# The first stage of four SwiGLU channel mixers by seven block products for eight, with the residual kept in DRAM between phases

## The chip, the cores and the metric

One Trainium2 chip, one core of it. The time is that of the device for one execution of the whole kernel, in microseconds (us); lower is better. TensorE (PE) multiplies, VectorE (DVE) and ScalarE (ACT) work element by element, GpSimd (POOL) does small things, and SyncE's queue (SP) issues the transfers between DRAM and the on-chip memory (SBUF). Products are summed in eight PSUM banks of 128 x 512 fp32.

## What is computed

Two layers of a trunk, each with a channel mixer, a token mixer and a second channel mixer. 640 tokens (512 latent, 128 context), width 1024, feed-forward width 2816:

```python
def _swiglu(x, w1, w3, w2):
    return (jax.nn.silu(x @ w1) * (x @ w3)) @ w2

def _layer(x, mod, l, norm_g, ffn_w1, ffn_w3, ffn_w2, mixer):
    sh1, sc1, g1, sh2, sc2, g2, sh3, sc3, g3 = jnp.split(mod[:, None, :].astype(x.dtype), N_MOD, axis=-1)
    h = _modulate(_rmsnorm(x, norm_g[l, 0]), sh1, sc1)
    x = x + 0.5 * g1 * _rmsnorm(_swiglu(h, ffn_w1[l, 0], ffn_w3[l, 0], ffn_w2[l, 0]), norm_g[l, 1])
    h = _modulate(_rmsnorm(x, norm_g[l, 2]), sh2, sc2)
    y, st = mixer(h)          # layer 0: recurrent (RG-LRU); layer 1: means over windows (pool)
    x = x + g2 * _rmsnorm(y, norm_g[l, 3])
    h = _modulate(_rmsnorm(x, norm_g[l, 4]), sh3, sc3)
    x = x + 0.5 * g3 * _rmsnorm(_swiglu(h, ffn_w1[l, 1], ffn_w3[l, 1], ffn_w2[l, 1]), norm_g[l, 5])
```

`mod` is a product of the conditioning vectors with a 1024 x 9216 matrix per layer. The weights are fp32 and are read once.

## The kernel before

The program is six phases in a row: FFN(0,0), RG(0,1), FFN(0,2), FFN(1,0), pool(1,1), FFN(1,2). FFN(l,s) is a channel mixer. The program is one stream of instructions for each engine, in the order in which the Python code writes them; engines wait for one another where data or buffers ask for it, and nothing reorders within an engine.

Every fp32 product is three products of the format fp32r: each operand is split into a high part (`wh`, `hh`, `gh`, a copy by ACT) and a low part (`wl`, `hl`, `gl`, a subtraction by DVE), and low x high, high x low and high x high are summed. Weights come in pieces of 128 x 1024 (512 KB) into two `raw` buffers and are split in `ensure` (ACT L137, DVE L138) into six `wh` and six `wl` slots, in the order in which they are used.

A channel mixer goes over 22 blocks of 128 feed-forward features. For a block, `ffn_A` makes u (with w1) and v (with w3), with the features on the 128 partitions, for token group A (256 tokens, bank `uvA`) and group B (384 tokens, banks `uB`, `vB`): eight input slices of 128, three products each (`mmA`, L326). `ffn_post` takes the silu of u (ACT) and multiplies by v (DVE, L347); `put_g` splits the result (L153, L154). After two blocks, `block_B` does the second stage with w2: five token tiles x two halves of the output, six products of 512 columns each into one of three `b` banks (`mmB`, L366), evacuated by DVE into `yacc` (L374). This is always one pair behind the first stage. The last four blocks are done tile by tile in `final`: behind each tile's last product come its norm, the residual `x` (`c_res`: L291, L292), the next phase's norm, transposes (PE L431), modulation (ACT L439, DVE L437) and the split into `hhA/hlA` (tiles 0 and 1) and `hhB/hlB` (tiles 2 to 4). `ffn_start` does the next phase's products for group A while the norms of the last tiles finish.

Between the products, `mod_step` slips in the products of the modulation for coming phases (PE L207, their weights in two `mw` buffers), and with `G` the vectors that scale the residual. `start` is the first phase's beginning, where the modulation comes in four groups of 256 features (PE L842) and products follow as each is there. The residual `x`, 640 x 1024, lies in SBUF; in the RG mixer, whose temporaries take its place, it is stored to DRAM and read back.

Of the kernel before, what the change touches and what calls it, by code (L numbers as in the profile page):

```python
# [16 lines left out]
P = 128  # L17
# [11 lines left out]
NW = 6  # L29
NRAW = 2  # L30
GAP = 2
SMP = TOK - P
XW = TOK + GAP

# Column table: name -> (first column, number of columns).
# [44 lines left out]
PAIRS = {1: (0, 1), 3: (2, 3), 4: (4,)}  # L80


class Kern:
    def __init__(self, ctx, tc, io):
# [8 lines left out]
    BUFS = {"wh": NW, "wl": NW, "raw": NRAW, "mw": 2, "yacc": NT, "gh": 4, "gl": 4,  # L93
            "xp": 1, "xc": 1, "r": 2, "i": 2, "a": 2, "gt": 1, "ab": 2, "G": 1,
            "st": 12, "uvA": 2, "uB": 1, "vB": 1, "b": 3, "m": 1}
# [9 lines left out]
    def init_pieces(self, pieces):  # L105
        self.pieces = pieces
        self.n_dma = 0
        self.n_split = 0
        self.raws = {}
        self.wparts = {}  # L110
        self.cur = 0
        self.limit = len(pieces)
        self.g_on_dve = False

    def dma_upto(self, n):
        while self.n_dma < min(n, len(self.pieces)):
            raw = self.t("raw", [P, D])
            self.nc.sync.dma_start(raw, self.pieces[self.n_dma])
            self.raws[self.n_dma] = raw
            self.n_dma += 1  # L120

    def ensure(self, last):
        last = min(last, self.limit - 1, len(self.pieces) - 1)
        while self.n_split <= last:
            i = self.n_split
            self.dma_upto(i + NRAW)
            raw = self.raws.pop(i)
            if i in self.scaled:
                for k in range(2):
                    rk = raw[:, k * 512:(k + 1) * 512]  # L130
                    self.nc.vector.tensor_mul(rk, rk, self.psc[self.scaled[i]])
            wh = self.t("wh", [P, D], F32R)
            wl = self.t("wl", [P, D], F32R)
            if self.dve_lo <= i < self.dve_hi:
                self.nc.vector.tensor_copy(wh, raw)
            else:
                self.nc.scalar.activation(wh, raw, AF.Copy)  # L137
            self.nc.vector.tensor_sub(wl, raw, wh.bitcast(F32))  # L138
            self.wparts[i] = (wh, wl)
            self.n_split += 1  # L140
        self.dma_upto(self.n_split + NRAW)

    def take(self):
        i = self.cur
        self.ensure(i)
        self.cur += 1
        return self.wparts.pop(i)

    def ahead(self, k=NW):
        self.ensure(self.cur + k - 1)  # L150
# [6 lines left out]
    def mod_init(self):  # L157
# [18 lines left out]
        self.m_use = 0  # L176
        self.ab = {}
# [5 lines left out]
    def mod_dma(self):  # L183
        while self.m_dma < min(self.m_use + 2, len(self.mitems)):
# [75 lines left out]
    def mod_step(self, n=1):  # L260
        for _ in range(n):
            if next(self.gen, "end") in ("hold", "end"):
                return

# [11 lines left out]
    def rstd(self, src):  # L276
        nc = self.nc
        junk = self.t("xp", [P, D], BF16)
# [6 lines left out]

    def c_res(self, t, l, s):
# [4 lines left out]
        nc.vector.scalar_tensor_tensor(y, y, rs, self.G[(l, s)][:, v], op0=ALU.mult, op1=ALU.mult)  # L291
        nc.vector.tensor_add(x, x, y)  # L292

    def c_stat2(self, t):
        self.rs2[t] = self.rstd(self.x[:, t])

    def c_xn(self, t):
        self.nc.scalar.activation(self.y[t], self.x[:, t], AF.Copy, scale=self.rs2[t])  # L298

    def c_T(self, t):  # L300
        self.tp[t] = []
        for h in range(2):
            pt = self.p("uB" if h == 0 else "vB")
            for q in range(4):
                kk = 4 * h + q
                self.nc.tensor.transpose(pt[:, q * P:(q + 1) * P], self.y[t][:, kk * P:(kk + 1) * P], self.col("ident"))
            self.tp[t].append(pt)

    def hsl(self, t):
        g, off = (0, t * P) if t < 2 else (1, (t - 2) * P)  # L310
        return g, slice(off, off + P)

    def new_h(self):
        self.hh = [self.t("hhA", [P, KC, 256], F32R), self.t("hhB", [P, KC, 384], F32R)]
        self.hl = [self.t("hlA", [P, KC, 256], F32R), self.t("hlB", [P, KC, 384], F32R)]
        self.rs2 = {}
        self.tp = {}

# [21 lines left out]
    def ffn_post(self, f, grp, u, v):  # L340
        nc = self.nc
        if grp == 0:
            self.su[f] = self.t("r", [P, XW])
# [678 lines left out]
```

## Time and profile before

| what | value |
|---|---|
| time, three runs | 2300.38, 2300.75, 2301.27 us (median 2300.75) |
| span of the profiled execution | 2297.5 us |
| the profiled execution's own time | not among the three; the median lies 3.25 us above the span |
| mean granted clock of TensorE | 0.992 |
| read from DRAM, written | 238.91 MB, 5.25 MB |

The span runs from the first to the last instruction. "Busy" is the sum of the durations of an engine's instructions where they don't overlap. The chain that ended last is followed back from the last instruction to whatever released it. In a group's row stand count, busy time, mean duration in ns of one, and then the idle time of the engine just ahead of these instructions with what ended most of it. In a timeline, chain or window row the first number is the start in us, the second the length.

### The profile page before, as it was taken

The numbers are of one execution on the slowest core, as the hardware profiler recorded it, in microseconds if no ns is written. First come the engines' busy times: TensorE is split into PE (matmuls) and PEld (weight loads), VectorE is DVE, ScalarE is ACT, GpSimd is POOL, SyncE is SP. The second block draws the span as 40 slices with busy tenths as digits, with TensorE's granted clock in tenths as the row PEclk, the third lists the DMA queues.
The fourth block names the chain that finished last, engine by engine and source line by source line (L and its number), as shares of the span: only waits on it lengthen the run. The fifth ranks groups of instructions, "written<-read, shape, count | busy, mean of one in ns | idle before, by whom it ended". The sixth has DMA issues, their size and how long they took to land.

```text
span 2297.5 us, 32647 instructions
## 1 busy us (share of the span) xinstructions
PE 2243.3 (98%) x14071; PEld 2024.6 (88%) x14071; DVE 1089.0 (47%) x1570; ACT 753.0 (33%) x1123; POOL 64.9 (3%) x107
## 2 busy tenths in 40 slices
PE   7999999998999999999999999999999899999998
PEld 5999889987888898989998898898897799999997
DVE  5333433346998643343344434334436743343444
ACT  5322112226976622112224421212125732222211
POOL 0000000000111000000000000000000100000000
PEclk9999999999999999999999999999999999999999
DMA  8333343324424344332221433433331322222221
GB/s 280 121 115 119 111 128 112 114 74 147 129 101 142 133 133 125 110 124 74 81 68 55 150 108 109 129 119 120 105 111 45 113 76 74 81 68 87 79 74 46
DMA packets 74288, 246.27 MB, mean 107 GB/s; under 512 B 7568, under 2 KB 15776, under 8 KB 74144
## 3 DMA queue, kind: packets, MB, share of 16 engines
q1 hardware_dynamic: 74112, 244.18, 33.6%
q8 instruction: 110, 1.80, 0.3%
q14 instruction: 34, 0.28, 0.0%
q0 software_dynamic: 32, 0.01, 0.0%
HBM read 238.91 MB, written 5.25 MB: 106 GB/s over the span
## 4 chain that ended last, share of the span: by engine, by line
PE 86%; DVE 6%; ACT 5%; DMA 2%; issue 1%; POOL 1%; SPq 0%; POOLq 0%; ACTq 0%; DVEq 0%
PE b L366 23%; PE uvA L326 22%; PE uB L326 17%; PE vB L326 16%; PE m L207 3%; ACT xp L280 2%; DVE yacc L291 1%; DVE x L292 1%; DVE yacc L374 1%; PE b L573 1%; POOL st L283 1%; DMA mw<-in_mod_w_dram 1%; ACT yacc L298 0%; PE b L746 0%; PE m L249 0%
## 5 line engine op out<-in xcount | busy, mean ns | idle before, releaser
L138 DVE TENSOR_TENSOR wl<-raw,wh 128x1024 fp32r<-128x1024 f32 x294 | 356.5, 1223 | 482.3 <-ACT wh L137 482.3
L137 ACT ACTIVATE wh<-raw 128x1024 fp32r<-128x1024 f32 x270 | 281.1, 1055 | 648.1 <-PE b L366 405.8
L326 PE MATMUL uvA<-hhA,wl 128*128 128x256 f32 x1536 | 440.2, 287 | 1.6 <-ACT xp L532 1.5
L326 PE MATMUL uvA<-hlA,wh 128*128 128x256 f32 x1536 | 435.8, 284 | 0.0
L326 PE MATMUL uvA<-hhA,wh 128*128 128x256 f32 x1536 | 435.3, 284 | 0.0
L366 PE MATMUL b<-wh,gl 128*128 128x512 f32 x960 | 376.6, 392 | 3.4 <-DVE gl L154 1.6
L366 PE MATMUL b<-wl,gh 128*128 128x512 f32 x960 | 375.0, 391 | 0.0
L366 PE MATMUL b<-wh,gh 128*128 128x512 f32 x960 | 374.3, 391 | 0.0
L374 DVE TENSOR_TENSOR yacc<-yacc,b 128x512 f32<-128x512 f32 x380 | 256.0, 686 | 169.7 <-PE b L366 169.6
L326 PEld LDWEIGHTS uvA<-hhA,wl 128*128 128x128 f32 x1536 | 294.3, 192 | 21.9 <-issue 15.4
L326 PEld LDWEIGHTS uvA<-hlA,wh 128*128 128x128 f32 x1536 | 294.8, 192 | 2.1 <-DVE hlB L154 0.4
L326 PEld LDWEIGHTS uvA<-hhA,wh 128*128 128x128 f32 x1536 | 294.7, 192 | 1.6 <-issue 1.6
L326 PE MATMUL uB<-hhB,wl 128*128 128x384 f32 x760 | 259.4, 341 | 0.9 <-ACT hhB L153 0.9
L326 PE MATMUL vB<-hhB,wl 128*128 128x384 f32 x760 | 254.8, 335 | 2.3 <-ACT gt L584 2.3
L326 PE MATMUL uB<-hlB,wh 128*128 128x384 f32 x760 | 254.9, 335 | 0.2
L326 PE MATMUL vB<-hhB,wh 128*128 128x384 f32 x760 | 255.0, 336 | 0.0
L326 PE MATMUL vB<-hlB,wh 128*128 128x384 f32 x760 | 254.9, 335 | 0.0
L326 PE MATMUL uB<-hhB,wh 128*128 128x384 f32 x760 | 254.6, 335 | 0.0
L366 PEld LDWEIGHTS b<-wh,gl 128*128 128x128 f32 x960 | 180.2, 188 | 48.0 <-issue 5.8
L366 PEld LDWEIGHTS b<-wh,gh 128*128 128x128 f32 x960 | 180.2, 188 | 37.6
L366 PEld LDWEIGHTS b<-wl,gh 128*128 128x128 f32 x960 | 180.3, 188 | 36.0
L347 DVE TENSOR_TENSOR r<-r,uvA 128x256 f32<-128x256 f32 x88 | 37.0, 421 | 266.6 <-ACT r L346 266.5
(207 smaller groups left out, 2389.5 us busy)
## 6 DMA issues: line engine op xcount, KB each, us to landing
raw<-in_w_dram SPq DMA_DIRECT2D x264, 512.0 KB, 3.5
mw<-in_mod_w_dram SPq DMA_DIRECT2D x132, 512.0 KB, 3.7
raw<-in_w_in_dram SPq DMA_DIRECT2D x16, 512.0 KB, 3.6
raw<-in_w_out_dram SPq DMA_DIRECT2D x8, 512.0 KB, 3.5
x_spill<-x SPq DMA_DIRECT2D x5, 512.0 KB, 2.6
x<-x_spill SPq DMA_DIRECT2D x5, 512.0 KB, 6.7
x<-in_x_s_dram SPq DMA_DIRECT2D x4, 512.0 KB, 6.3
wl<-in_mod_w_dram SPq DMA_DIRECT2D x4, 512.0 KB, 9.0
```

The costliest lines, as they stand in the source:

```text
L137: self.nc.scalar.activation(wh, raw, AF.Copy)
L138: self.nc.vector.tensor_sub(wl, raw, wh.bitcast(F32))
L207: nc.tensor.matmul(ps[32 * j:32 * j + 32, 0:256], self.csil[:, k, :], w[:, j * 256:(j + 1) * 256], start=(k == 0), stop=(k == KC - 1), til ...
L280: nc.scalar.activation(junk, src, AF.Square, scale=1.0 / 32.0, accum_out=ms)
L283: nc.gpsimd.tensor_tensor(rs, ms, self.mhalf, op=ALU.pow)
L291: nc.vector.scalar_tensor_tensor(y, y, rs, self.G[(l, s)][:, v], op0=ALU.mult, op1=ALU.mult)
L292: nc.vector.tensor_add(x, x, y)
L326: self.nc.tensor.matmul(out, a[:, sl], b[g][:, k], start=(n == 0), stop=(n == 3 * KC - 1))
L347: nc.vector.tensor_mul(su[:, cs], su[:, cs], v)
L366: nc.tensor.matmul(pb, a[:, ts_], b[:, ns], start=(c == 0), stop=(c == 3 * len(fl) - 1))
L374: nc.vector.tensor_add(y, y, pb)
L573: nc.tensor.matmul(pb, u[:, ws], v[:, a:b], start=(n == 0), stop=(n == 2))
```

## The change

**The block products.** Two blocks of features are taken together. Tokens are halved (320 and 320, `HT`), input features are halved (512 and 512, `HK` = 4 slices), and the two blocks of a pair are the halves of the output. With A the 2 x 2 blocks of the token matrix and b those of the weight, the four output blocks of u (and of v) come from seven products in Winograd's form of Strassen's algorithm, each of 4 slices x 3 fp32r products of 320 columns: A11 b11, A12 b21, S1 t1, S2 t2, S3 t3, S4 b22, A22 t4, with

    S1 = A21 + A22    S3 = A11 - A21    S2 = S1 - A11    S4 = A12 - S2
    t1 = b12 - b11    t3 = b22 - b12    t2 = b22 - t1    t4 = t2 - b21

(Line numbers of the changed kernel are added behind some lines.) The S are made once a phase, by DVE, and split (`h_sums`, L410 to L413 and L207/L208). The t are made for each weight by DVE (`weight_gen`), and each of the seven operands is split by itself, as a quarter of 128 x 512 (ACT L136, DVE L137), into 11 `wp` slots that hold high and low part together. A weight of a pair now comes as one load of 1 MB; w2 comes in pairs of blocks, 1 MB, split as before (L174, L177). The products are combined by DVE from PSUM.

```diff
+                b11, b12, b22, b21 = (raw[:, n * 512:(n + 1) * 512] for n in range(4))
+                if kind == "full":
+                    yield quarter(b11)
+                T = self.t("T", [P, D])
+                t1, t3 = T[:, 0:512], T[:, 512:D]
+                V.tensor_sub(T, raw[:, 512:1536], raw[:, 0:1024])      # L150
+                t2, t4 = b12, b11
+                V.tensor_sub(t2, b22, t1)                              # L152
+                yield quarter(t2)
+                if kind == "full":
+                    yield quarter(b21)
+                yield quarter(t3)
+                yield quarter(t1)
+                V.tensor_sub(t4, t2, b21)                              # L158
+                yield quarter(t4)
+                yield quarter(b22)
...
+    def h_sums(self, ks, cols):
+        V = self.nc.vector
+        (f11, f12), (f21, f22), s1 = *([x[:, ks, cols] for x in f] for f in self.F), self.fs1[:, ks, cols]
+        V.tensor_add(s1, f21, f22)
+        V.tensor_sub(f21, f11, f21)
+        V.tensor_sub(f11, s1, f11)
+        V.tensor_sub(f12, f12, f11)
+        for n, x in (("S2", f11), ("S3", f21), ("S1", s1), ("S4", f12), ("A22", f22)):
+            hi, lo = self.H[n]
+            self.split(hi[:, ks, cols], lo[:, ks, cols], x)
...
+    def prod(self, out, h, **kw):
+        self.mmP(out, h, self.get(), **kw)      # 12 matmuls, L472
+        self.done()                             # makes the next quarters, as slots allow
+
+    def seven_rest(self, u, s1, tag):
+        V = self.nc.vector
+        c12, c21, c22 = u[:, 1, 0:HT], u[:, 0, HT:TOK], u[:, 1, HT:TOK]
+        p6 = self.bank(tag)
+        self.prod(p6, "S2")
+        V.tensor_add(c12, p6, s1)               # L497
+        yield
+        p7 = self.bank(tag)
+        self.prod(p7, "S3")
+        V.tensor_add(c21, p7, c12)              # L501
+        p5 = self.bank(tag)
+        self.prod(p5, "S1")
+        V.tensor_add(c22, p5, c21)              # L504
+        p4 = self.bank(tag)
+        self.prod(p4, "A22")
+        V.tensor_sub(c21, c21, p4)              # L507
+        self.prod(p5, "S4", onto=True)
+        V.tensor_add(c12, c12, p5)              # L509
+        yield
+
+    def seven(self, u):
+        p1 = self.bank()
+        self.prod(p1, "A11")
+        s1 = u[:, 0, 0:HT]
+        self.nc.scalar.activation(s1, p1, AF.Copy)   # L517
+        it = self.seven_rest(u, s1, "q")
+        next(it)
+        self.prod(p1, "A12", onto=True)
+        next(it)
+        return p1
```

`onto` adds to a bank that holds a sum already. Four `q` banks and three `b` banks take the place of `uvA`, `uB`, `vB` and `b`. `ffn_u` takes the silu (ACT L530 of the first output block, L531 of the other three), `ffn_v` multiplies (DVE L536, L537) and splits g (L207, L208, 1280 elements for the pair). The second stage's matmuls and evacuations (L561) are as before.

**The phases.** `ffn_start` does A11 and A12 of the first two pairs' four weights and copies the results of A11 aside; the other five products of each need all tokens. `ffn_rest` does these (for the first pair into `b` banks), the second stage of the first pair, and from the third pair on the whole:

```diff
+    def ffn_start(self, nxt):
+        self.mod_allow(self.phase_mods[nxt[0:2]])
+        self.ffn_open()
+        for m in range(4):
+            self.prod(self.c11[m], "A11")
+            self.nc.scalar.activation(self.s1[m], self.c11[m], AF.Copy)
+        self.mod_step(5)
+        for m in range(4):
+            self.prod(self.c11[m], "A12", onto=True)
+        self.mod_step(4)
+        self.ahead()
...
+        for b in range(2, NB):
+            u, v = self.ffn_uv(b)
+            self.ffn_u(u, self.seven(u))
+            self.mod_step(2)
+            self.ffn_v(b, u, v, self.seven(v))
+            self.mod_step(2)
+            if b < NB - 1:
+                self.block_B((2 * b - 2, 2 * b - 1), False)
+                self.mod_step(2)
```

**The residual.** `x` has no place in SBUF any more. `c_res` loads a token tile of it from DRAM into one of the two `mw` buffers (a tile ahead), and `c_next` stores it back, in every phase. Because `mw` is shared, `mod_allow` caps how far the modulation runs ahead.

```diff
     def c_res(self, t, l, s):
         nc = self.nc
-        y, x = self.y[t], self.x[:, t]
+        if t == 0:
+            self.xt = {}
+            self.x_load(0)
+        if t + 1 < NT:
+            self.x_load(t + 1)
+        y, x = self.y[t], self.xt[t]
```

RG and pool use the new buffers, and RG takes tokens in groups of 320 and 320 instead of 256 and 384. `start` works in the same four groups of modulation with the new operands.

**The order on the engines.** VectorE in one steady pair of FFN(1,0), from the weights of the pair's first block to that block's g. Before, weight splits (L138) take turns with the multiplications by v (L347) and the split of g (L154):

```order
L138 TENSOR_TENSOR wl_12051<-raw_11968,wh_12050 128x1024
L347 TENSOR_TENSOR r_12041<-r_12041,uvA_11992 128x256
L138 TENSOR_TENSOR wl_12177<-raw_12048,wh_12176 128x1024
L347 TENSOR_TENSOR r_12041<-r_12041,vB_12063 128x384
L138 TENSOR_TENSOR wl_12183<-raw_12054,wh_12182 128x1024
L154 TENSOR_TENSOR gl_12115<-r_12041,gh_12114 128x640
```

One weight split stands ahead of each reader of a bank (`uvA`, `vB`). After, in a steady pair of the same phase, the combinations of u (L501 to L509) stand between weight sums (L150, L152, L158) and splits of quarters (L137) and of w2 (L177):

```order
L137 TENSOR_TENSOR wp_13157<-raw_12874,wp_13157 128x512
L501 TENSOR_TENSOR c_13108<-q_13160,c_13108 128x320
L177 TENSOR_TENSOR wp_13191<-raw_13077,wp_13175 128x1024
L504 TENSOR_TENSOR c_13108<-q_13178,c_13108 128x320
L507 TENSOR_TENSOR c_13108<-c_13108,q_13194 128x320
L150 TENSOR_TENSOR T_13271<-raw_13173 128x1024
L177 TENSOR_TENSOR wp_13222<-raw_13077,wp_13207 128x1024
L509 TENSOR_TENSOR c_13108<-c_13108,q_13178 128x320
L152 TENSOR_TENSOR raw_13173<-raw_13173,T_13271 128x512
```

The readers of PSUM (L504, L509) now have rows of 1024 elements directly ahead of them.

ScalarE in the same pair, after (L136 and L174 are high parts of weights, L531 the silu of three output blocks, L517 the copy of v's A11):

```order
L174 ACTIVATE wp_13175<-raw_13077 128x1024
L174 ACTIVATE wp_13207<-raw_13077 128x1024
L531 ACTIVATE c_13108<-c_13108 128x960
L136 ACTIVATE wp_13254<-raw_13173 128x512
L517 ACTIVATE c_13109<-q_13239 128x320
```

The copy that v's A12 waits for stands behind the silu of u.

VectorE at the beginning of FFN(1,0), where the last token tile's operands are made. Before, the split of the last tiles (`hlB`) is followed by the weight splits and multiplications of the phase:

```order
L437 TENSOR_SCALAR i_10931<-vB_10930,ab_7603 128x128 x4
L154 TENSOR_TENSOR hlB_10622<-i_10919,hhB_10620 128x4x128
L154 TENSOR_TENSOR hlB_10622<-i_10931,hhB_10620 128x4x128
L138 TENSOR_TENSOR wl_11251<-raw_10970,wh_11250 128x1024
L347 TENSOR_TENSOR r_11027<-r_11027,vB_11139 128x384
```

After, the sums and five splits of the last tile alone (the columns of 128), and then the weight work that stands ahead of the first combination, L497:

```order
L410 TENSOR_TENSOR g_10872<-g_10870,g_10871 128x4x128
L208 TENSOR_TENSOR h_10867<-g_10871,h_10866 128x4x128
L411 TENSOR_TENSOR g_10870<-c_10868,g_10870 128x4x128
L208 TENSOR_TENSOR h_10863<-g_10872,h_10862 128x4x128
L412 TENSOR_TENSOR c_10868<-g_10872,c_10868 128x4x128
L208 TENSOR_TENSOR h_10861<-g_10870,h_10860 128x4x128
L413 TENSOR_TENSOR c_10869<-c_10869,c_10868 128x4x128
L208 TENSOR_TENSOR h_10859<-c_10868,h_10858 128x4x128
L137 TENSOR_TENSOR wp_11238<-raw_11219,wp_11238 128x512
L208 TENSOR_TENSOR h_10865<-c_10869,h_10864 128x4x128
L137 TENSOR_TENSOR wp_11241<-T_11235,wp_11241 128x512
L137 TENSOR_TENSOR wp_11244<-T_11235,wp_11244 128x512
```

Two rows a tile have become nine, and in the order in which S2 (`h_10859`) comes fourth.

More of the change, by code (lines that the diff above doesn't have):

```diff
@@ L33 @@
 XW = TOK + GAP
+HT = TOK // 2
+HK = KC // 2
 COLS = {}
@@ L143, in take, with load_upto @@
[L143 to L150, printed above, removed]
+        self.made = []
+        self.live = 0
+        self.stop_at = len(entries)
+        self.wgen = self.weight_gen()
+    def load_upto(self, n):
+        while self.n_load < min(n, len(self.entries)):
+            kind, srcs = self.entries[self.n_load][:2]
+            raw = self.t("raw", [P, 2 * D])
+            w = 2 * D // len(srcs)
+            for i, s in enumerate(srcs):
+                self.nc.sync.dma_start(raw[:, i * w:(i + 1) * w], s)
+            self.raws[self.n_load] = raw
+            self.n_load += 1
@@ new lines, in make, with get, done, ahead @@
+    def make(self):
+        w = next(self.wgen, None)
+        if w is None:
+            return False
+        self.made.append(w)
+        self.live += 1
+        return True
+    def get(self):
+        while not self.made:
+            assert self.make()
+        return self.made.pop(0)
+    def done(self, n=1, room=0):
+        self.live -= n
+        self.ahead(room)
+    def ahead(self, room=0):
+        while self.live < NWP - room:
+            if not self.make():
+                return
@@ L309, in hsl, with c_next @@
-    def hsl(self, t):
-        g, off = (0, t * P) if t < 2 else (1, (t - 2) * P)
-        return g, slice(off, off + P)
-    def new_h(self):
[L314 to L317, printed above, removed]
-    def mmA(self, out, w, g, ks=range(KC)):
+    def c_next(self, t, l, s, plain):
+        x = self.xt.pop(t)
+        rs = self.rstd(x, self.y[t])
+        self.nc.scalar.activation(self.y[t], x, AF.Copy, scale=rs)
+        self.nc.sync.dma_start(self.spill[:, t], x)
+        if t in PAIRS:
+            self.c_h(PAIRS[t], l, s, plain)
@@ new lines, in mmP @@
+    def mmP(self, out, h, w, ks=range(HK), start=True, stop=True, first=0, last=HK - 1, onto=False):
+        hi, lo = self.H[h]
+        for k in ks:
+            wh, wl = w[:, k * P:(k + 1) * P], w[:, 512 + k * P:512 + (k + 1) * P]
+            for n, (a, b) in enumerate(((wl, hi), (wh, lo), (wh, hi))):
+                self.nc.tensor.matmul(out, a, b[:, k], start=(start and not onto and k == first and n == 0), stop=(stop and k == last and n == 2),
+                                      skip_group_check=onto)
@@ L357, in mmB, with ffn_v @@
+    def ffn_v(self, b, u, v, c11):
+        V = self.nc.vector
+        fu, fv = u.rearrange("p f t -> p (f t)"), v.rearrange("p f t -> p (f t)")
+        V.tensor_mul(fu[:, 0:HT], fu[:, 0:HT], c11)
+        V.tensor_mul(fu[:, HT:2 * TOK], fu[:, HT:2 * TOK], fv[:, HT:2 * TOK])
+        gh = self.t("g", [P, 2, TOK], F32R)
+        gl = self.t("g", [P, 2, TOK], F32R)
+        self.split(gh, gl, u)
+        for i in range(2):
+            self.g[2 * b + i] = (gh[:, i], gl[:, i])
     def mmB(self, t, n, fl, ws, first):
@@ L377, in new_y, with block_B @@
         self.y = [self.t("yacc", [P, D]) for _ in range(NT)]
-    def block_B(self, fl, first):
-        ws = [self.take() for _ in fl]
+    def block_B(self, fl, first, room=0):
+        ws = [self.pair() for _ in fl]
         for t in range(NT):
@@ L383, in block_B @@
                 self.mmB(t, n, fl, ws, first)
-            if t in (1, 3):
-                self.ahead(NW - 3 + t // 2)
         for f in fl:
             del self.g[f]
+        self.done(2 * len(fl), room)
     def final(self, fl, l, s, nxt, start_next):
-        ws = [self.take() for _ in fl]
+        ws = [self.pair() for _ in fl]
         if nxt:
-            self.new_h()
+            (self.new_plain if nxt[2] else self.new_h)()
         for t in range(NT):
@@ new lines, in ffn_open @@
+    def ffn_open(self):
+        self.g = {}
+        s1 = self.t("yacc", [P, D])
+        self.c11 = [self.bank() for _ in range(4)]
+        self.s1 = [s1[:, m * HT:(m + 1) * HT] for m in range(3)] + [self.t("yacc", [P, D])[:, 0:HT]]
+    def ffn_start(self, nxt):
+        self.mod_allow(self.phase_mods[nxt[0:2]])
[7 more added lines that the diff above has]
+        self.mod_step(4)
+        self.ahead()
@@ L677, in rg_rest @@
             if c >= 1:
-                self.rg_gate(c - 1, self.take())
-                self.ahead(3)
+                self.rg_gate(c - 1, self.pair())
+                self.done(2, 4)
                 self.rg_y(c - 1)
```

591 lines of the change are left out of this document (306 added, 285 removed).

## The prediction, made before the changed kernel was run

> **What bounds the kernel now.** First the page: engine totals, the chain that ended last, the costliest groups, the loads.
>
> ```profile
> PE 2243.3 (98%) x14071; PEld 2024.6 (88%) x14071; DVE 1089.0 (47%) x1570; ACT 753.0 (33%) x1123; POOL 64.9 (3%) x107
> ...
> PE b L366 23%; PE uvA L326 22%; PE uB L326 17%; PE vB L326 16%; PE m L207 3%; ACT xp L280 2%; DVE yacc L291 1%; DVE x L292 1%; DVE yacc L374 1%; PE b L573 1%; POOL st L283 1%; DMA mw<-in_mod_w_dram 1%; ACT yacc L298 0%; PE b L746 0%; PE m L249 0%
> ...
> L138 DVE TENSOR_TENSOR wl<-raw,wh 128x1024 fp32r<-128x1024 f32 x294 | 356.5, 1223 | 482.3 <-ACT wh L137 482.3
> ...
> L374 DVE TENSOR_TENSOR yacc<-yacc,b 128x512 f32<-128x512 f32 x380 | 256.0, 686 | 169.7 <-PE b L366 169.6
> ...
> raw<-in_w_dram SPq DMA_DIRECT2D x264, 512.0 KB, 3.5
> ```
>
> TensorE (PE) is the bound: busy in 98%, its matmuls 78% of the chain in four first- and second-stage rows. VectorE (DVE) has half its time free. The chain of waits in an undisturbed stretch of FFN(1,2) gives the pitch of one pair of FF blocks:
>
> ```profile
> 2176.46 13.67 PE b L366 x60
> 2190.12 5.75 PE uvA L326 x48
> 2195.88 4.16 PE uB L326 x24
> 2200.04 4.16 PE vB L326 x24
> 2204.20 5.75 PE uvA L326 x48
> 2209.95 4.16 PE uB L326 x24
> 2214.12 4.16 PE vB L326 x24
> 2218.28 13.68 PE b L366 x60
> ```
>
> No piece but matmuls, end to end. The pitch is 2218.28 - 2176.46 = 41.82 us: 13.67 second stage, 28.15 first stage, with steps of 4.16/24 = 0.1733 us for 384 columns, 5.75/48 = 0.1198 for 256 and 13.67/60 = 0.2278 for 512. So the step is linear in the columns, 0.000422 us each and 0.012 fixed. The timeline of the RG mixer has the new width itself:
>
> ```profile
> 600.96 0.31 PE L573 MATMUL b<-wh,wl 128*128 128x320 f32 x1
> 601.10 0.31 PE L573 MATMUL b<-wl,wh 128*128 128x320 f32 x1
> 601.25 0.31 PE L573 MATMUL b<-wh,wh 128*128 128x320 f32 x1
> 601.40 0.33 PE L326 MATMUL vB<-hhB,wl 128*128 128x384 f32 x1
> ```
>
> Start to start: (601.40 - 600.96)/3 = 0.1467 us for 320.
>
> **TensorE's own part.** Per pair the change issues 2 x 7 products of 12 matmuls, 168 x 0.1467 = 24.65 us for 28.15: 3.50 less, pitch 38.32 if nothing waits. Four phases of 11 pairs: 44 x 3.50 = -154 us. The RG mixer's groups of 320 and 320 instead of 256 and 384 cost 2 x 0.1467 = 0.2934 for 0.2931 per product step: nothing, in the open. Transposes, modulations and the second stage are the same in number.
>
> **DVE's part.** Its durations overlap where steps stand back to back:
>
> ```profile
> 1150.66 1.88 DVE L374 TENSOR_TENSOR yacc<-yacc,b 128x512 f32<-128x512 f32 x3
> 1161.97 2.35 DVE L138 TENSOR_TENSOR wl<-raw,wh 128x1024 fp32r<-128x1024 f32 x2
> ```
>
> Three of 0.686 take 1.88, two of 1.223 take 2.35. So the step is (1.88-0.686)/2 = 0.60 us for 512 and 2.35-1.223 = 1.13 for 1024; between them 0.065 + 0.00104 per element: 0.40 for 320, 1.07 for 960, 1.40 for 1280. The Trainium skill, "VectorE: DVE Perf Modes", section "The DRAIN you can't avoid", says that the next operation does not start until the pipe of the last has emptied. The two rows show a step about 0.09 us shorter than the duration, so whole durations would overstate; by that rule the steady ledger below would be some 31 us instead of 28.8, and still under the pitch.
>
> A steady pair now asks of DVE: 14 quarter splits of 512 (8.4), two weight sums T of 1024 (2.3), four of 512 (2.4), two second-stage splits (2.3), ten combinations of 320 (4.0), the two multiplications (1.5), the split of g (1.4), ten evacuations (6.0): 28.3, and 28.8 with the modulations' small steps, of 38.3. Before it was six splits of 1024, four multiplications, two splits of 640 and ten evacuations, 16. So DVE stays below TensorE in a steady pair, 75%, but it is no longer loose: results of TensorE stand in its queue behind weight work, and most of it lies in the 24.65 us of the first stage. How fast one engine answers another:
>
> ```profile
> 1160.94 0.39 PE L366 MATMUL b<-wh,gh 128*128 128x512 f32 x1
> 1161.16 0.28 PE L326 MATMUL uvA<-hhA,wl 128*128 128x256 f32 x1
> 1161.36 0.69 DVE L374 TENSOR_TENSOR yacc<-yacc,b 128x512 f32<-128x512 f32 x1 [0.67 <-PE b L366]
> ```
>
> The last B matmul gives way at 1161.16 and its evacuation starts at 1161.36: 0.20 us.
>
> **A steady pair walked through**, t = 0 where the second stage ends, a product being 1.76 us (12 x 0.1467). (1) u's products run A11, S2, A12, S3, S1, A22 to 10.57. S4 adds to S1's bank, so it waits for L504, the reader of that bank. S1 is done at 8.81, but ahead of L504 stands L177, the 1024 split of a second-stage weight whose slot comes free just then: 9.0 to 10.13, L504 to 10.62. S4 is late by 0.15. (2) The raw weights come as 1 MB instead of 512 KB; the 3.5 us of the page's row become between 3.5 and 7.0, I take 5.3 (estimate: two pieces in parallel share what one leaves idle). The buffer frees at about 6.9, so T (L150) cannot start before 12.1; behind it are the next L177 and L509. ACT's silu (L531) waits for L509, behind it a quarter copy, behind that the copy of v's A11 (L517), which v's A12 needs: 0.25 to 0.85 late. (3) In the second stage the split of g stands between two evacuations and waits for ACT's copy of 1280 elements; three banks cover 4 us: 0 to 0.9. Sum 0.4 to 1.9; with modulation steps on the same queues nearer the top. I take 1.5 per pair: 36 steady pairs x (3.50 - 1.5) = -72 us. Bounds: stalls of 0.3 and 2.5 give -115 and -36. SP's queue carries the same bytes in half as many issues; the x tiles share it and the two `mw` buffers, of which the next part.
>
> **The four starts.** Where a phase begins, before goes from its first product on new tokens to the first second stage:
>
> ```profile
> 1262.07 0.28 PE L326 MATMUL uvA<-hhA,wl 128*128 128x256 f32 x1
> ...
> 1282.35 0.38 PE L326 MATMUL uB<-hhB,wl 128*128 128x384 f32 x1
> ```
>
> ```profile
> 1331.59 3.44 PE b L366 x15
> ```
>
> That is 69.5 us from 1262.07, of which 20.3 go by until the last tokens' products can start. What DVE does in those 20 us is mostly waiting for norms:
>
> ```profile
> 1268.57 1.28 DVE L291 SCALAR_TENSOR_TENSOR yacc<-yacc,st,G 128x1024 f32<-128x1024 f32 x1 [0.96 <-POOL st L283]
> ...
> 1278.59 0.69 DVE L154 TENSOR_TENSOR hlB<-i,hhB 128x512 fp32r<-128x512 f32 x1 [1.24 <-ACT hhB L153]
> ```
>
> After, its queue from the same point to the split of the last S2, the first of the five operands that need all tokens, is 44 rows: 11 splits of tokens 7.4, 8 sums 5.8, 5 quarter splits 3.0, two residual additions and a scaling 3.5, T and a weight sum 1.7, 12 modulations 2.4, an evacuation 0.6, small ones 0.2: 24.6, and with 3 to 5 of the waits just shown about 29. TensorE's cover is only the eight A11 and A12 products (14.1), transposes and modulations (5): it idles some 10 us. Then come 20 products, 35.2 us of TensorE, against 38 to 42 us of DVE rows up to the last combination of the second pair, the first 10 of them weight work ahead of the first evacuation (L497), with three `b` banks. So TensorE follows DVE: 29 + 42 + 3 = 74 us to the first second stage for 69.5. FFN(0,2) and FFN(1,0): +5 each (0 to +10).
>
> FFN(1,2) starts behind the pool, whose tail covers nothing: the sums and splits of the last tiles lie bare, and the vector G of the pool's residual comes later since its loads share `mw` with x: +15 (5 to 25). Phase FFN(0,0):
>
> ```profile
> 47.51 1.43 PE m L842 x24
> ...
> 61.97 11.51 PE uvA L326 x96
> ...
> 98.73 4.31 PE b L366 x18
> ```
>
> Its first second stage at 98.73 comes 36.8 us after the last modulated features. After, the sums on the token side begin with the third of four modulation groups (estimate: 43, some 5 us before the fourth's product at 47.51), and about 60 us of DVE rows stand between there and the first second stage: 103, and 110 with waits for the last group's features. +11 (0 to 20). Last, the clock. The columns are the stretch, its length, busy times of PE, PEld, DVE, ACT and POOL, granted clock, DMA share, GB/s:
>
> ```profile
> 1806.00:1812.00 6.00, 2.28 (x19) 0.40 (x16) 5.11 (x9) 4.39 (x7) 1.98 (x2) 0.71 0.65 189
> 1812.00:1818.00 6.00, 5.19 (x21) 2.84 (x22) 3.96 (x7) 4.22 (x10) 0.55 (x1) 0.50 0.84 337
> ```
>
> After a stretch in which PE was busy 2.28 of 6 us, the next ran at 0.50 of the clock. Three starts that newly idle lose about 2 us each (1 to 3 from half of 6 us): +6. The Trainium skill, "TensorE: Matmul & The Clock Gate", section "Why this matters for your kernels", says that idle gaps over about 3 us put the clock back to half; the two rows agree. That rule speaks against this change only at the starts, since no steady stall above reaches 1 us.
>
> RG and pool inside: other buffer names, same products, covered by the chain they had: 0 (-3 to +3). Sum of the starts 5 + 5 + 15 + 11 + 6 = +42, taken as +40.
>
> **Sum.** -72 + 40 = -32. The profiled execution has a span of 2297.5 us; the median of the three runs is 2300.75, 3.25 above it, an offset that I leave. 2300.75 - 32 = 2268.
>
> **Rivals.** (a) TensorE stays gapless in the steady pairs: 36 x 3.50 = 126 less, starts as above: 2300.75 - 126 + 40 = 2215; with starts hidden as well, -154: 2147. For it: DVE is at 75% and matmuls run pair to pair without a hole now. Against: the queue order in (1) and (2), where each hole follows from a row. (b) DVE's queue sets the steady pitch: if each of the five combinations per product group is late by 0.3 rather than the few named, 10 x 0.3 = 3 and the 0.3 of (3) make 3.3 per pair. Gain 36 x 0.2 = 7 against 40: 2334, slower. It decides from a stall of 3.50 - 40/36 = 2.4 us per pair. For it: in u's part 10.8 of 12.3 us of DVE's queue are filled, and one late row is handed on to the next. Against: four `q` banks, so that most products may end 1.7 us before their reader. (c) The starts cost 10 and not 40: 2300.75 - 72 + 10 = 2239. For it: DVE idles there now; against: the 24.6 us counted. (d) The short holes themselves bring the clock down: one drop a pair at half of 6 us is 36 x 3 = +108, about 2375. No row here shows holes under 1 us with a low clock, so it gets little. The Trainium skill, "TensorE: Matmul & The Clock Gate", section "A second HAM failure mode: psum-queue depth-cycling", says that frequent micro-idles between groups through cycling banks can do this. That the seven products are not issued is excluded: the changed code's matmuls of 320 columns count 7392 = 44 x 168.
>
> **How the numbers follow.** Less than 0.2% (4.6 us) I call no change, about what can be told apart here. Chances: the forecast 0.50 (its own range 2240 to 2302, of which 0.05 within no change), (a) 0.18, of which 0.04 for all hidden, (c) 0.09, (b) 0.20, (d) 0.03. Faster 0.45 + 0.18 + 0.09 = 0.72, same 0.05 and a hundredth of (b), slower 0.22. The range 2205 to 2330 leaves out (a) all hidden, (d) and the upper part of (b).
>
> **What the profile after would show.** Steps of 0.147 in the rows of 320; pairs of 39.5 to 40.2 us with waits of PE on DVE L504 and ACT L517 in each; DVE near 1720 us, 75% of the span; PE near 2090; at the starts PE waiting 8 to 12 us for DVE's token splits, and a clock under 1 behind them. Wrong would be: pairs at 38.3 (a), pairs above 41 (b), a low clock between starts (d), first second stages no later than before (c).

## The result: 1.7% faster, as forecast in sum, by two terms that were wrong in opposite directions

The changed kernel takes 2261.8 us in the median of four runs (2258.65 to 2265.16), before 2300.57: a ratio of 0.9833, 95% interval 0.9819 to 0.9847. The forecast was 2268. The profiled execution took 2265.16 us, with a span of 2263.4 for 2297.5: 34.1 less. It is the slowest of the four, 3.4 us over the median, and its starts of FFN(0,0) and FFN(1,0) are up to 2.5 and 2.9 us longer than in profiles of other kernels that are alike there; a difference of that size in these two starts is not read as an effect below.

The page of the changed kernel, the lines that answer to those of before:

```profile
PE 2114.6 (93%) x13015; PEld 1894.6 (84%) x13015; DVE 1688.3 (75%) x2604; ACT 979.9 (43%) x1555; POOL 78.2 (3%) x107
...
PE 75%; DVE 10%; ACT 6%; DMA 5%; issue 2%; POOL 1%; SPq 1%; POOLq 0%; ACTq 0%; DVEq 0%
...
raw<-in_w_dram SPq DMA_DIRECT2D x88, 1024.0 KB, 4.8
```

TensorE has 129 us less to do and the span is only 34 shorter: 93% busy for 98%. VectorE stands at 75% of the span, as forecast. In a steady pair of FFN(1,2) it is busy 30.30 of 38.62 us, 78%, where the ledger had 28.8 of 38.3 (stretch, length, PE, PEld, DVE, ACT, POOL, granted clock, DMA share, GB/s):

```profile
2069.94:2108.56 38.62, 38.62 (x230) 35.95 (x229) 30.30 (x46) 13.68 (x21) 0.00 (x0) 1.00 0.24 83
```

The chain of waits in FFN(1,2) shows where nothing was lost:

```profile
2083.75 24.97 PE q L472 x168
2108.72 13.65 PE b L553 x60
2122.37 24.96 PE q L472 x168
2147.34 13.65 PE b L553 x60
```

No piece but matmuls. The pitch is 38.62 us for 41.82 before: 3.20 less of the 3.50 that the matmuls alone give. So the waiting is in the starts, and the table of TensorE's waits (total, times, longest) names it. Before, for the same three kinds:

```profile
PE uB L431 <- ACT yacc L298: 7.5, 12, 2.0
PE m L207 <- DMA mw<-in_mod_w_dram: 5.1, 6, 3.2
PE uB L306 <- ACT yacc L298: 11.2, 3, 9.8
```

After:

```profile
PE q L430 <- ACT yacc L382: 67.6, 16, 9.5
PE m L262 <- DMA mw<-in_mod_w_dram: 22.3, 19, 3.7
PE b L979 <- ACT yacc L974: 12.6, 3, 10.8
```

L430 are the transposes of the next phase's tokens, L382 the scaling of a tile after its second norm; this wait grew from 7.5 to 67.6 us. The third row belongs to the very first start and hardly changed. Cut at the first and last second-stage matmul of each phase, the two spans compare so (us; worked out from the matmuls' starts):

| stretch | before | after | difference | forecast |
|---|---|---|---|---|
| FFN(0,0), up to its first second stage | 98.7 | 115.0 | +16.3 | +13 |
| RG, whole | 242.9 | 253.7 | +10.8 | 0 |
| start of FFN(0,2) | 69.0 | 88.7 | +19.8 | +7 |
| start of FFN(1,0) | 69.4 | 83.1 | +13.7 | +7 |
| pool and start of FFN(1,2) | 118.7 | 154.4 | +35.7 | +15 |
| four channel mixers, first second stage to last | 1688.7 | 1557.5 | -131.1 | -72 |
| end | 10.2 | 10.9 | +0.7 | 0 |

The prediction does not say which three starts lose its 6 us for the clock; they are put on the first, third and fourth rows here. The steady part gave 59 more than forecast, the rest cost 55 more. Of the -131, 36 pitches of 3.20 are 115; 160 modulation matmuls, of 0.57 us for eight, moved out of these stretches into the starts (11 us); the rest is small. One stretch repeats to about 3 us only: the start of FFN(1,0) took 83.1 here, and 80.7 and 80.2 in the kernels of runs 7 and 4, which are alike there.

### The profile page after: what moved, and what is told of

It is laid out like the page before. It is cut to its first block, busy times and chain, and to the rows that moved or that the text cites. A ratio compares the mean times of both kernels' runs of the same rounds, so it can differ in the third digit from the quotient of the medians.

```text
span 2263.4 us, 32357 instructions
## 1 busy us (share of the span) xinstructions
PE 2114.6 (93%) x13015; PEld 1894.6 (84%) x13015; DVE 1688.3 (75%) x2604; ACT 979.9 (43%) x1555; POOL 78.2 (3%) x107
## 4 chain that ended last, share of the span: by engine, by line
PE 75%; DVE 10%; ACT 6%; DMA 5%; issue 2%; POOL 1%; SPq 1%; POOLq 0%; ACTq 0%; DVEq 0%
PE q L472 43%; PE b L553 24%; PE m L262 2%; PE b L472 2%; DMA mw<-in_mod_w_dram 2%; DMA raw<-in_w_dram 2%; PE q L481 2%; DVE mw L377 2%; POOL st L352 1%; DVE yacc L376 1%; DVE wp L177 1%; DVE h L776 1%; ACT h L738 1%; DVE h L208 1%; DVE wp L137 1%
## 5 line engine op out<-in xcount | busy, mean ns | idle before, releaser
L472 PE MATMUL q<-h,wp 128*128 128x320 f32 x6912 | 1049.7, 312 | 6.0 <-DVE c L504 2.6
L472 PEld LDWEIGHTS q<-h,wp 128*128 128x128 f32 x6912 | 1024.1, 189 | 35.4 <-issue 15.2
L553 PE MATMUL b<-wp,g 128*128 128x512 f32 x2880 | 670.6, 392 | 2.8 <-DVE g L208 2.0
L553 PEld LDWEIGHTS b<-wp,g 128*128 128x128 f32 x2880 | 537.7, 188 | 120.9 <-issue 6.2
L136 ACT ACTIVATE wp<-raw 128x512 fp32r<-128x512 f32 x440 | 267.6, 628 | 636.5 <-PE b L553 294.3
L137 DVE TENSOR_TENSOR wp<-raw,wp 128x512 fp32r<-128x512 f32 x440 | 298.1, 689 | 107.0 <-ACT wp L136 106.2
L561 DVE TENSOR_TENSOR yacc<-yacc,b 128x512 f32<-128x512 f32 x380 | 258.3, 685 | 119.4 <-PE b L553 117.3
L177 DVE TENSOR_TENSOR wp<-raw,wp 128x1024 fp32r<-128x1024 f32 x118 | 144.2, 1223 | 69.7 <-PE q L472 59.5
L174 ACT ACTIVATE wp<-raw 128x1024 fp32r<-128x1024 f32 x94 | 99.6, 1061 | 151.2 <-PE q L472 143.3
L136 ACT ACTIVATE wp<-T 128x512 fp32r<-128x512 f32 x176 | 109.3, 627 | 104.2 <-PE q L472 103.3
L137 DVE TENSOR_TENSOR wp<-T,wp 128x512 fp32r<-128x512 f32 x176 | 118.0, 689 | 14.4 <-ACT wp L136 14.2
L150 DVE TENSOR_TENSOR T<-raw 128x1024 f32<-128x1024 f32 x88 | 107.7, 1224 | 26.7 <-DMA raw<-in_w_dram 25.4
L481 PE MATMUL q<-h,wp 128*128 128x320 f32 x768 | 123.6, 316 | 2.2 <-DVE wp L177 2.2
L481 PEld LDWEIGHTS q<-h,wp 128*128 128x128 f32 x768 | 116.2, 191 | 9.9 <-issue 4.9
L262 PE MATMUL m<-mw,csil 128*32 128x256 f32 x1024 | 85.3, 402 | 23.2 <-DMA mw<-in_mod_w_dram 22.3
L430 PE MATMUL q<-cols,yacc 128*128 128x128 f32 x200 | 38.1, 351 | 67.9 <-ACT yacc L382 67.6
L430 PEld LDWEIGHTS q<-cols,yacc 128*128 128x128 f32 x200 | 30.3, 181 | 78.4 <-ACT yacc L382 78.0
L207 ACT ACTIVATE g<-c 128x1280 fp32r<-128x1280 f32 x44 | 56.2, 1277 | 71.8 <-DVE c L537 71.5
L208 DVE TENSOR_TENSOR g<-c,g 128x1280 fp32r<-128x1280 f32 x44 | 65.5, 1488 | 10.0 <-ACT g L207 9.7
```

Of the source, the lines that this page charges most:

```text
L136: nc.scalar.activation(w[:, 0:512], src, AF.Copy)
L137: V.tensor_sub(w[:, 512:D], src, w[:, 0:512].bitcast(F32))
L150: V.tensor_sub(T, raw[:, 512:1536], raw[:, 0:1024])
L174: nc.scalar.activation(wh, r, AF.Copy)
L177: V.tensor_sub(wl, r, wh.bitcast(F32))
L208: self.nc.vector.tensor_sub(lo, src, hi.bitcast(F32))
```

## Experiments

Each ratio is to the kernel before, on the same chip, with its 95% interval; the changed kernel has 0.9833. Differences by stretch are of profiled spans.

**1. Products ahead of the last tile's transposes.** In the trace the reason for the 67.6 us seemed the order in TensorE's queue. Before, products of the next phase run from the first moment, between transposes (the start of FFN(1,0); in that of FFN(0,2), too, the first product follows the last second-stage matmul at once):

```profile
1262.07 0.28 PE L326 MATMUL uvA<-hhA,wl 128*128 128x256 f32 x1
1262.19 0.27 PE L431 MATMUL uB<-cols,yacc 128*128 128x128 f32 x1
1262.30 0.27 PE L431 MATMUL vB<-cols,yacc 128*128 128x128 f32 x1
1262.33 0.36 PE L326 MATMUL uvA<-hlA,wh 128*128 128x256 f32 x1
```

After (the timeline of TensorE in the start of FFN(0,2), whose last second-stage matmul ends at 761.9), the first product comes behind the last transpose:

```profile
782.21 1.08 PE L262 MATMUL m<-mw,csil 128*32 128x256 f32 x8 [3.64 <-DMA mw<-in_mod_w_dram]
787.61 1.97 PE L430 MATMUL q<-cols,yacc 128*128 128x128 f32 x8 [4.32 <-ACT yacc L382]
789.23 1.15 PE L472 MATMUL q<-h,wp 128*128 128x320 f32 x3
```

That is 27.3 us after the last second-stage matmul; in the start of FFN(1,0) it is 18.6. In the run the last tile's transposes, which then go to `b` banks, stand behind the four A11 products.

```diff
-        if t in PAIRS:
+        if t == 4 and not plain:
+            self.late = (PAIRS[t], l, s, plain, "b")
+        elif t in PAIRS:
...
             self.prod(self.c11[m], "A11")
             self.nc.scalar.activation(self.s1[m], self.c11[m], AF.Copy)
+        self.c_h(*self.late)
```

> The changed kernel with the last token tile's transposes put behind the four A11 products of the next phase and into the b banks. Theory 'queue order': at the starts TensorE waits 67.6 us for scaled tiles (ACT L382) in front of transposes, while the A11 products, which need only the first 320 tokens, stand behind them in its queue and share the q banks with them; moved ahead they fill 7 us of that at each of the starts of FFN(0,2), FFN(1,0) and FFN(1,2): 18 to 24 us less, 2238 to 2244 for 2262. Theory 'VectorE chain': the five operands that need all tokens come when VectorE has made them; the same products only run earlier and TensorE waits later: within 4 us of 2262. Theory 'mw buffers' (residual and modulation weights share two buffers): within 4 us as well.

Ratio 0.9783 (0.9767 to 0.9798), 2249.39 us. The three starts got 4.3, 2.9 and 3.4 us shorter, half of what the queue order promised, and the 2.9 of FFN(1,0) lie within the scatter of that stretch; the span is 10.5 less. It is one cause and not the main one. A11 still stands behind the transposes of tiles 2 and 3 here: its first product comes 15.4 us after the last second-stage matmul in FFN(0,2).

**2. No modulation in the starts.**

```diff
-        self.mod_step(5)
...
-        self.mod_step(4)
```

> The changed kernel without the nine modulation steps in the channel mixers' starts; they run later in the phase, between the pairs. Theory 'mw buffers': their weights cannot load while the residual's tiles hold the two mw buffers, and TensorE's 22.3 us of waits for them (L262 on DMA mw, 19.9 of them in the three starts) go: 12 to 20 us less, 2242 to 2250. Theory 'VectorE chain': TensorE waits for VectorE's operands instead: within 4 us of 2262. Theory 'queue order': within 4 us.

Ratio 0.9825 (0.9806 to 0.9844), 2259.32 us: no difference that can be told. The three starts got 5.6, 6.9 and 6.1 us shorter, the bodies of FFN(0,2), FFN(1,0) and FFN(1,2), where the steps now run, 5.7, 6.4 and 1.3 longer. Of the waits for modulation weights, 19.9 us in the starts, no more than the 2.5 us between the medians comes back. The theory of the `mw` buffers is wrong in this form.

**3. The residual alone.** The kernel before, with `x` loaded from DRAM and stored back for each tile and phase, and the modulation capped as in the change:

```diff
-        y, x = self.y[t], self.x[:, t]
+        if t == 0:
+            self.xt = {}
+            self.x_load(0)
+        if t + 1 < NT:
+            self.x_load(t + 1)
+        y, x = self.y[t], self.xt[t]
...
-        while self.m_dma < min(self.m_use + 2, len(self.mitems)):
+        while self.m_dma < min(self.m_use + 2, self.m_cap):
```

> The kernel before with one part of the change alone: the residual in DRAM between phases, loaded a tile ahead into the two mw buffers, and the cap on the modulation steps. Theory 'mw buffers': the modulation's weights come late at the starts: +6 to +20 us, 2307 to 2321 for 2300.6. Theories 'queue order' and 'VectorE chain': the residual costs nothing by itself, -2 to +4.

Ratio 1.0146 (1.0129 to 1.0163), 2333.29 us: 33.7 slower, beyond every expectation. By stretch: RG +12.3, start of FFN(0,2) +4.3, pool and start of FFN(1,2) +23.2, FFN(0,0) -5.5, the rest under 1. Before, the modulation ran ahead freely, and the scale G of the pool's residual was ready when the pool began. The chain of waits of this kernel, inside the pool:

```profile
1803.50 0.60 PE m L207 x7
1804.11 3.64 DMA mw<-in_mod_w_dram
1807.76 0.04 issue
1807.80 0.68 PE m L207 x8
1808.50 5.92 DMA mw<-in_mod_w_dram
1814.42 0.04 issue
1814.47 0.64 PE m L207 x8
```

Each 512 KB of weights waits for one of two buffers, is multiplied in 0.6 us, and the next load comes 3.6 to 5.9 us later. The residual of the pool's first tile waits for the end of that chain: it is at 1831.0, 55.2 us after FFN(1,0)'s last product, for 33.6 before.

**4. The pool's scale early.** The eight products of that scale done at the end of FFN(1,0), in the changed kernel:

```diff
-(1, 0): [(1, 0, 2), (1, 1, 0), (1, 1, 1), (1, 2, 0), (1, 2, 1)],
+(1, 0): [(1, 0, 2), (1, 1, 0), (1, 1, 1), (1, 2, 0), (1, 2, 1), (1, 1, 2)],
...
         for m in self.phase_mods[l, s]:
-            self.mod_until(*m)
+            if m == (1, 1, 2):
+                while next(self.gen) != "hold":
+                    pass
+                self.held = True
+            else:
+                self.mod_until(*m)
```

> The changed kernel with the eight modulation products of the pool's residual scale (1,1,2) done at the end of FFN(1,0), where the kernel before has them, and not inside the pool. Theory 'cap' (sharing the mw buffers forced these products into the pool's uncovered tail; the residual alone cost 23.2 us there): the stretch from the end of FFN(1,0) to the first second stage of FFN(1,2) gets 10 to 18 us shorter, FFN(1,0) 4 to 5 longer: 2249 to 2256 for 2262. If that stretch is set by the norms of the pool's tiles or by VectorE's sums alone: within 3 us of 2262.

Until G's buffer is free the generator stops at "hold", and the first norm's scratch tile moves from `mhl` to `T` meanwhile. Ratio 0.9793 (0.9777 to 0.9809), 2250.87 us. Pool and start of FFN(1,2) 15.0 shorter, FFN(1,0) 5.8 longer: as the theory of the cap says.

**5. No sums.** The four token-side sums left out, 5.8 us of VectorE's steps at each start:

```diff
-        V.tensor_add(s1, f21, f22)
-        V.tensor_sub(f21, f11, f21)
-        V.tensor_sub(f11, s1, f11)
-        V.tensor_sub(f12, f12, f11)
...
```

> The changed kernel without the four sums of the token side (S1 to S4 are not formed; the five splits stay, of other data, so the output is another): 5.8 us less of VectorE's steps at each start, nothing else. Theory 'VectorE chain' (the first run moved products ahead and got 10.6 us of span for the 21 us that the queue order promised, so something else holds the rest): the five operands come 4 to 6 us sooner at each of the four starts, 15 to 22 us in all, 2240 to 2247 for 2262. Theory 'norm chain' (the last tiles' norms and residuals through ScalarE and GpSimd, one tile after the other, set the time): within 4 us of 2262.

Ratio 0.9793 (0.9779 to 0.9808), 2252.77 us, between the two theories: FFN(0,0) 7.8 shorter (kernels with an unchanged beginning were 0.6 to 2.5 shorter too, so 5 to 7), FFN(0,2) 3.8, the others 0.2 and 1.2. VectorE's sums set the first start; at the others they mostly lie beside another wait.

**6. No second norm.** Which wait sets the other starts? The second norm of each tile is left out, and x is scaled by the first norm's factor instead.

```diff
+        self.rs1 = rs
...
-        rs = self.rstd(x, self.y[t])
+        rs = self.rs1
```

> The changed kernel with the second norm of each token tile left out (x is scaled by the first norm's factor, so the output is another): ScalarE's square with its accumulator, one GpSimd step and the crossings between them go, about 3 us of each tile's latency, 5 tiles at each of five boundaries; no product and no split changes. Theory 'norm chain' (TensorE's 67.6 us in front of the transposes are the latency of the last tiles' norms): 3 to 5 us less at each of the five boundaries, 12 to 25 in all, 2237 to 2250 for 2262. Theory 'VectorE chain' (VectorE's queue full from the last second-stage product on): at most 1 us at each, within 5 us of 2262.

Ratio 0.9732 (0.9716 to 0.9748), 2236.89 us: 25 faster than the changed kernel by the medians (23 by the ratios), with not one product, sum or split less. Start of FFN(0,2) 11.3 shorter, pool and FFN(1,2) 15.3, RG 2.4; FFN(1,0) 0.7 only. TensorE's wait in front of the transposes fell from 67.6 us:

```profile
PE q L431 <- ACT yacc L383: 41.7, 21, 7.4
```

So the starts of FFN(0,2) and FFN(1,2) hang on the latency of the last tiles' norms, through four engines, tile after tile. That chain was there before, and by the trace of before the products on group A, the first two tiles, covered it from its first moment, with modulation steps among them; no run takes the norm out of the kernel before. Now A11 needs half of the third tile, which is transposed with the fourth, and the cover begins when the chain is nearly over.

In FFN(1,0) the first product comes 7.6 us sooner in this run, and the first second stage only 0.7. Its chain of waits, behind the tokens' splits, runs over a load of weights that takes 8.17 us and goes out 0.4 us behind one for the modulation:

```profile
1254.48 1.12 DVE T L150
1255.60 8.17 DMA raw<-in_w_dram
1263.86 0.60 DVE T L150
```

So there another wait ends nearly as late as the norms. No run takes that load's delay away alone.

**7. VectorE's slack.** T made once, twice or four times more for the weights of some pairs of FFN(1,2), in one execution:

```diff
-                V.tensor_sub(T, raw[:, 512:1536], raw[:, 0:1024])
+                for _ in range(1 + (opt or 0)):
+                    V.tensor_sub(T, raw[:, 512:1536], raw[:, 0:1024])
...
```

> The changed kernel with the weight sum T of FFN(1,2) made several times over: one more for each weight of pairs 4 and 5, two more for 6 and 7, four more for 8 and 9 (2.3, 4.5 and 9.0 us of VectorE a pair). The pitch there is 38.62 us, VectorE's steps by the prediction's ledger 28.8. If VectorE's queue order sets the pitch (the prediction's stalls of 1.5 a pair, rival b), each dose lengthens it: +1 or more at the first, +3 at the second, +8 at the third. If it only has to stay below TensorE in sum, 38.6 to 38.8 at the first two doses (31.1 and 33.3) and a rise at the third alone (37.8 of 38.6, +0.5 to +3).

From second stage to second stage the pitches are 38.61, 38.63, 38.63, 38.63, 38.70, 38.68, 38.45, 36.62 and 41.33 us, with the doses rising along them. The first two doses cost under 0.1; the third shows in the last two, which with their two predecessors make 155.08 for 4 x 38.62 = 154.48. The whole stretch took 376.3 us for 376.2. VectorE in two pairs under the second dose and the third (stretch, length, PE, PEld, DVE, ACT, POOL, granted clock):

```profile
2067.80:2106.48 38.68, 38.68 (x231) 35.95 (x229) 34.07 (x49) 13.21 (x21) 0.00 (x0) 1.00 0.23 82
2106.48:2144.93 38.45, 38.45 (x231) 35.97 (x230) 35.57 (x50) 10.63 (x16) 0.00 (x0) 1.00 0.23 82
```

At 34.07 and 35.57 of some 38.5, 88 and 93%, TensorE is still busy throughout; the third dose costs 0.6 us in sum over four pairs. In a steady pair VectorE has to fit in sum, and rows added at this place of its queue cost next to nothing; other places were not tried.

**8. Together.** Products first, and token tiles 2 and 3 each transposed by itself, meant to free A11 from waiting for tile 3:

```diff
+APART = {1: (0, 1), 2: (2,), 3: (3,), 4: (4,)}
...
+        elif t in (PAIRS if plain else APART):
+            self.c_h((PAIRS if plain else APART)[t], l, s, plain)
```

> As the run with the products first, and token tiles 2 and 3 are transposed, modulated and split each by itself rather than as a pair, so that A11, which needs half of tile 2, does not wait for tile 3's norm. Theory 'queue order': A11 comes a tile's norm (6 us) sooner and fills TensorE's wait: 9 to 18 us less than the 2249.4 of that run, 2231 to 2240. Theory 'VectorE chain': the five other operands are not sooner, and more small rows stand in VectorE's queue: 2248 to 2256.

Ratio 0.9793 (0.9778 to 0.9807), 2251.93 us: nothing over products first alone (0.9783). But the edit does not free A11. In the trace of the next kernel, which has it too, the start of FFN(0,2) shows tile 2's transposes, then a wait of 9.80 us for tile 3's, which stand ahead of A11 in TensorE's queue, and only then the first product:

```profile
762.02 1.09 PE L433 MATMUL q<-cols,yacc 128*128 128x128 f32 x8 [2.37 <-ACT yacc L383]
772.92 1.97 PE L433 MATMUL q<-cols,yacc 128*128 128x128 f32 x8 [9.80 <-ACT yacc L383]
774.54 1.68 PE L475 MATMUL q<-h,wp 128*128 128x320 f32 x5
```

That is 15.0 us after the last second-stage matmul, where products first alone has 15.4. So what an A11 free of tile 3 would give stays untested. From the changed kernel's 27.3 the first product comes 12.3 sooner, and yet the first second stage only 5.6: the other five operands still wait for the last tile. With the pool's scale early as well:

> Products first, tiles apart and the pool's scale early, together. If each works by itself they add: the run before this one less 6 to 13 us. If both only move the same wait, no faster than the better of the two.

Ratio 0.9756 (0.9742 to 0.9771), 2243.66 us: the two add. And without modulation steps in the starts, with the tiles apart and as a pair:

> Products first, tiles apart, the pool's scale early, and no modulation steps in the channel mixers' starts. Alone, taking these steps out changed nothing (2.5 us within the scatter), and the run with the other three had a ratio of 0.9756. In that run TensorE still waits 9.4 us for modulation weights at the starts. Theory 'one wait hides the other': now that the products come sooner, the weights' waits lie open, and without them 5 to 10 us go: ratio 0.971 to 0.9735. Theory 'VectorE chain': no change, ratio 0.9745 to 0.9765.

> As the first of this group, but with tiles 2 and 3 still transposed as a pair. If splitting them gains nothing (the run with tiles apart was within the scatter of the run with the products first alone), the same ratio as that kernel within 0.0015; if an earlier A11 pays now that nothing else stands in front, 0.002 to 0.005 more.

0.9777 (0.9763 to 0.9792) and 0.9756 (0.9741 to 0.9770). The first lies above both of its expectations: without the steps the kernel with tiles apart is not faster but some 5 us slower, so they are no hidden wait there either. Why it is slower was not looked into. The second was expected at the first's ratio or above it, and is 0.0021 below. In this form, with A11 behind tile 3 all the same, tiles apart do not pay. The best of these, 0.9756, is 55 us faster than the kernel before and 18 than the changed one.

## Why the prediction was right in sum, point by point

**TensorE's own part** was right in the steady pairs, where steps of 320 columns take 0.147 us. Over the span it is 129 us less busy, for 154; the mean clock is 0.967 for 0.992, which lengthens the matmuls at the starts, and the difference was not split further.

**The steady pair: the mechanism right, the size wrong.** The forecast stall was 1.5 us, chosen near the top of 0.4 to 1.9. It is 38.62 - 38.32 = 0.30. The walk was nearly exact where it was a walk. In FFN(1,2), from the end of a second stage, L177 starts at 9.07 (forecast 9.0) and L504 at 10.21 (10.13); from start to start S4's first two matmuls lose 0.12 us (0.15). The raw weights land 4.65 us after their issue at 6.91, not 5.3, so T starts at 11.58 (12.1), and everything behind it comes half a microsecond sooner:

```profile
2136.22 0.48 DVE L509 TENSOR_TENSOR c<-c,q 128x320 f32<-128x320 f32 x1
...
2137.18 0.99 ACT L531 ACTIVATE c<-c 128x960 f32<-128x960 f32 x1
...
2138.07 0.42 ACT L517 ACTIVATE c<-q 128x320 f32<-128x320 f32 x1
```

In this phase the quarter's copy stands ahead of the silu and not behind it, and L517 ends at 2138.49, just when A12 is due: 0.17 lost for 0.25 to 0.85. The split of g held no matmul up here. Three holes were each judged above their size because the rows behind them looked full; the dose run shows that they had room, although VectorE was busier than the ledger said. The step that failed is "Sum 0.4 to 1.9 ... I take 1.5 per pair". Rival (a), which had 0.18, was the right one for the steady part.

**The starts: the named cause right in kind, two terms missing.** "TensorE's cover is only the eight A11 and A12 products ... it idles some 10 us" failed: in the start of FFN(0,2) the cover came after the idling, and five waits of 20.3 us in all stand ahead of the first product. The code and the order showed why, and were not read: A11's last 64 tokens come with the pair of tiles 2 and 3, and the transposes take the `q` banks that the products need next. The opening text also says that each engine's stream has the order of the Python code; the trace of before shows otherwise, since products stand between transposes that the code writes first. From the last second-stage matmul the window rows, in the same columns, show TensorE busy for 0.74, 3.46 and 5.47 of 10 us each and its clock down to 0.50:

```profile
762.00:772.00 10.00, 0.74 (x5) 0.42 (x4) 9.30 (x17) 6.84 (x12) 2.57 (x4) 0.68 0.67 238
772.00:782.00 10.00, 3.46 (x20) 2.58 (x20) 9.56 (x18) 6.75 (x16) 0.92 (x1) 0.67 0.58 207
782.00:792.00 10.00, 5.47 (x26) 4.59 (x27) 6.53 (x10) 5.70 (x9) 3.74 (x1) 0.50 0.44 145
```

The Trainium skill, "TensorE: Matmul & The Clock Gate", section "Why this matters for your kernels", has idle gaps over about 3 us put the clock back to half; these rows agree. Rival (d) did not come: the clock stands at 1.00 in the steady pairs, whose holes are 0.1 us.

"RG and pool inside ... 0 (-3 to +3)" failed by about 10 us in RG and the pool's +15 by 21. The residual was priced as bytes on SP's queue and a later G. Measured alone (run 3) it costs 34 us: 40 in the stretches that lost 96, and 6 back in FFN(0,0), whose modulation moved out. How it costs 12 of them in RG was not taken apart. What is left of the 96, 56, is the block products' side, if the two add, for which about 40 was forecast: nearer, though partly for a wrong reason.

**The sum** then came out at 2262 for 2268 by luck: by the profiled spans a gain forecast 59 too small met a cost forecast 55 too small. Either error alone would have put it at 2209 or at 2323, outside the forecast's own range of 2240 to 2302, though not outside the wide one of 2205 to 2330. (The starts were added up to 42 and taken as 40, and 2300.75 - 32 is 2268.75: neither matters here.)

**Left open.** How much of the start of FFN(1,0) is the weight load that run 6 lays bare, what an A11 ahead of tile 3's transposes would bring, and what the remaining 7 to 9 us of the first start are, besides the sums (5 to 7) and some 2.3 us of modulation steps moved there.

## What to carry to other kernels

A loop whose engine is busy end to end takes a cut in its work nearly whole, as long as the next engine fits in sum: at 78% busy, with single rows late, it cost 0.3 us in 38.6 here, and up to 93% another 0.6 over four pairs. Look for the price at the seams: ask of every product meant as cover which tokens its operands need and what stands ahead of it in its own queue. And price a shared buffer by the loads that it stops from running ahead, at another place of the program, not by its bytes.

## What the runs showed of the hardware that was not expected

GpSimd's norm step on 128 x 1 elements takes 0.55 us in most places, and 3.74 in the start of FFN(0,2), while VectorE runs instructions on SBUF operands back to back, one of them already under way:

```profile
782.41 0.68 DVE L137 TENSOR_TENSOR wp<-T,wp 128x512 fp32r<-128x512 f32 x1
782.64 3.74 POOL L352 TENSOR_TENSOR st<-st,mhalf 128x1 f32<-128x1 f32 x1 [9.72 <-DVE st L350]
783.01 0.95 DVE L413 TENSOR_TENSOR c<-c,c 128x768 f32<-128x768 f32 x1
783.88 0.95 DVE L208 TENSOR_TENSOR h<-c,h 128x768 fp32r<-128x768 f32 x1
784.75 1.22 DVE L150 TENSOR_TENSOR T<-raw 128x1024 f32<-128x1024 f32 x1
786.41 1.15 ACT L382 ACTIVATE yacc<-mw,st 128x1024 f32<-128x1024 f32 x1 [3.10 <-POOL st L352]
```

It ends 0.4 us after the last of them. The Trainium skill, "GPSIMD Engine Reference", section "Specifications", says that GpSimd shares its SBUF interfaces with VectorE and contends with instructions that have two SBUF inputs; the rows agree, and give its size. Beside evacuations, whose second input is in PSUM, it keeps its 0.55. Of its 60 executions 10 took over 0.8 us, 16.1 us together, for 3 of before. All ten stand beside a VectorE instruction with two SBUF inputs. Since the tile's scaling waits for it, VectorE's extra work here also lengthens the norm chain of run 6. So does its queue: the two steps of the last tile's residual stand apart by 4.6 us of other rows, the modulation, splits and a sum of tiles 2 and 3:

```profile
772.95 1.28 DVE L376 SCALAR_TENSOR_TENSOR yacc<-yacc,st,G 128x1024 f32<-128x1024 f32 x1 [0.44 <-POOL st L352]
...
778.87 1.22 DVE L377 TENSOR_TENSOR mw<-mw,yacc 128x1024 f32<-128x1024 f32 x1
```

How much of the 25 us either is was not separated.
